# Weight sums made by adding transfers in DRAM, a new order of first use, and a last product cut in column halves

## The chip, the cores and the metric

The kernel runs on one core of one Trainium2 chip. TensorE multiplies, VectorE (DVE), ScalarE (ACT) and GpSimd (POOL) work on tiles in the on-chip memory, SyncE (SP) issues most transfers. The metric is the device time of one execution in microseconds; the median of 3 runs is 2372.4 (2371.81 to 2376.11).

## The reference

One decoder layer on 512 tokens, model width 2048, in float32:

```
h = RMSNorm(x); z = h @ W_in          # q, k, v of 8 attention heads; q, k, v, gate of 8 retention heads
a = block-sparse causal attention (QK-RMSNorm, rotary);  r = silu(gate) * groupnorm(retention)
x += concat(a, r) @ W_o
x += (silu(h2 @ W_gate) * (h2 @ W_up)) @ W_down      # h2 = RMSNorm(x), inner width 5632
x += (p @ W_pp) * sigmoid(RMSNorm(x) @ W_pg + b_pg)
```

## The kernel before

Every product keeps float32 accuracy by splitting each operand into a rounded part H and a rest L (`split`, L51: ScalarE makes H, VectorE makes L) and multiplying three times (`mm3`, L72: H by H, H by L, L by H).

The large products after the first go through seven multiplications of half-size blocks instead of eight. A `Group` (L245) computes 512 rows by 1024 columns over 2 to 4 units of depth 512. Its seven products come in the order of `ORDER` (L112): 1, 5, 6, 3, 7, 2, 4. One step is one product of one unit: 12 matmuls of 512 columns. The weight side of each product is a quarter of the weights or a sum of quarters: product 1 uses quarter 11; 5 is 11 + 12; 6 adds 22; 3 uses 22; 7 is 12 + 22; 2 uses 21; 4 adds 21 to the sum of 6. `add` (L269) makes these sums on VectorE in place, in the tile `raw` of 128 x 1024 numbers, by `plus` (L80, the group "raw<-raw" of L81). So a unit has four loads of 512 KB and four sums. The activation side of each product, its "factors" (`factors`, L173), is made on VectorE and ScalarE from transposed chunks, and either stays in tiles s and r or is spilled to DRAM through the four buffers of the tile o (`spill`, L194) and reloaded (`reload`, L225).

`run` (L148) goes through the list of steps; at step i it calls `extract` (the split) for step i + 2, `add` for step i + 3 and `multiply` for step i. Tile places the instructions on each engine by a simulation of its own, except where `keep_in_program_order` pins them. The raw tiles have three tags of four buffers each (l1, bd, c). The split tiles wh and wl have three buffers.

In order of time: the head (about 0 to 53 us by the trace), where class `Plain` (L452) multiplies the first q and k columns directly while x is loaded, scaled and split (`h_chunk` L499, `first_factors` L506, driven by `beside` L543); three groups for the values and gates; the mixer (about 285 to 720 us), where the projections of the heads run beside attention and retention, with one call of `weights` (L610) per unit of depth 256; two groups with W_o; eleven groups gu0 to gu10 with W_gate and W_up (L1025; gu0's first steps go unit by unit, in the order of `in_units`, because its factors are only being made); six groups with W_down in three parts of depth (L1031), the last part with 3 units; and two groups with W_pg (L1073; called pl0 and pl1 here). `evacuate` (L320) brings results out of the accumulation banks X, Y, Z; `gate` (L1050) finishes the output. Twenty idle matmuls on zeros (L449) stand before the first real one.

## Time and profile before

| | us |
|---|---|
| median of the three runs | 2372.4 |
| the profiled execution: its span, first to last instruction | 2367.2 |
| TensorE busy in it | 2317.0 |
| VectorE busy | 1943.3 |
| ScalarE busy | 1197.7 |
| GpSimd busy | 61.9 |

The profile is one execution; "busy" counts the time in which at least one instruction of the engine ran. Matmuls are pipelined, so TensorE can be busy and yet not at its peak. What waits for what is read from the semaphores; a wait is put down to what came last.

### The profile page before, as it was taken

The page shows a single profiled execution, that of the slowest core. Times are in us where ns is not written, and L with a number is a line of the kernel's source. Part 1 is how long each engine was busy: PE and PEld are TensorE (multiplying, and loading weights), DVE is VectorE, ACT ScalarE, POOL GpSimd, SP SyncE. Part 2 cuts the span into 40 slices and gives each one's busy share as a digit, 9 for nine tenths or more (in the row PEclk, how much of TensorE's full clock was granted, in tenths as well). Part 3 has the DMA queues.
Part 4 walks back from the last instruction along what each step waited for, and adds up shares of the span by engine and source line. Part 5 has one row for each costly group of instructions (what it writes and reads, how often), then busy time and mean ns, then how long its engine had stood idle before and what let it go on. Part 6 is the DMA issues. An engine that isn't in the chain of part 4 may idle for free.

```text
span 2367.2 us, 29161 instructions
## 1 busy us (share of the span) xinstructions
PE 2317.0 (98%) x10480; PEld 1898.7 (80%) x10480; DVE 1943.3 (82%) x2626; ACT 1197.7 (51%) x1791; POOL 61.9 (3%) x47
## 2 busy tenths in 40 slices
PE   9999999999999999999999999999999999999898
PEld 7888877788877877888888888888888878887777
DVE  8888686666667998888988898888888878789997
ACT  7644454444455565544554455445544434356653
POOL 0000011100010002000000000000000000000000
PEclk9999999999999999999999999999999999999999
DMA  6634733345666694346434643464577856857463
GB/s 233 241 130 162 233 104 123 129 149 182 195 216 257 231 346 160 109 163 201 147 111 156 200 152 111 151 200 155 204 322 253 290 219 235 331 183 259 137 204 124
DMA packets 166529, 456.26 MB, mean 193 GB/s; under 512 B 18544, under 2 KB 31216, under 8 KB 162288
## 3 DMA queue, kind: packets, MB, share of 16 engines
q1 hardware_dynamic: 162400, 446.00, 55.3%
q10 hardware_dynamic: 2704, 4.20, 0.7%
q0 software_dynamic: 1280, 4.20, 0.5%
q8 instruction: 82, 1.34, 0.2%
q14 instruction: 63, 0.52, 0.1%
HBM read 348.42 MB, written 101.71 MB: 190 GB/s over the span
## 4 chain that ended last, share of the span: by engine, by line
issue 57%; PE 26%; DVE 10%; DMA 5%; ACT 1%; POOL 1%; SPq 0%; ACTq 0%; POOLq 0%; DVEq 0%
PE acc L63 10%; PE Y L63 6%; PE Z L63 4%; DVE wl L55 3%; PE at L63 3%; DVE raw L81 2%; PE X L63 2%; DMA h<-o 1%; ACT wh L54 1%; PE tp L68 1%; DMA pp<-pp 1%; POOL rstd L84 1%; DMA s<-h 0%; DMA mix<-o 0%; DVE o L55 0%
## 5 line engine op out<-in xcount | busy, mean ns | idle before, releaser
L54 ACT ACTIVATE wh<-raw 128x1024 fp32r<-128x1024 f32 (+1 forms) x728 | 769.5, 1059 | 866.0 <-PE Y L63 307.8
L55 DVE TENSOR_TENSOR wl<-raw,wh 128x1024 fp32r<-128x1024 f32 (+1 forms) x728 | 884.4, 1218 | 281.4 <-ACT wh L54 280.5
L63 PE MATMUL Y<-wh,s 128*128 128x512 f32 x1656 | 525.6, 391 | 5.5 <-DVE v L78 3.2
L81 DVE TENSOR_TENSOR raw<-raw 128x1024 f32<-128x1024 f32 x376 | 453.2, 1217 | 20.1 <-DMA raw<-in_w_gu 7.2
L63 PEld LDWEIGHTS Y<-wh,s 128*128 128x128 f32 x1656 | 310.9, 188 | 72.9 <-ACT wh L54 5.4
L63 PE MATMUL Z<-wh,s 128*128 128x512 f32 x1152 | 365.1, 390 | 0.3 <-ACT wh L54 0.2
L63 PE MATMUL X<-wh,s 128*128 128x512 f32 x1008 | 320.9, 392 | 7.5 <-ACT wh L54 4.7
L63 PE MATMUL Y<-wl,s 128*128 128x512 f32 x828 | 324.8, 392 | 1.1 <-DVE wl L55 0.9
L63 PEld LDWEIGHTS Z<-wh,s 128*128 128x128 f32 x1152 | 216.2, 188 | 45.6 <-ACT wh L54 1.2
L63 PE MATMUL Z<-wl,s 128*128 128x512 f32 x576 | 228.0, 396 | 4.5 <-DVE wl L55 4.5
L63 PEld LDWEIGHTS X<-wh,s 128*128 128x128 f32 x1008 | 189.6, 189 | 49.1 <-ACT wh L54 6.7
L63 PE MATMUL X<-wl,s 128*128 128x512 f32 x504 | 197.8, 392 | 0.8 <-DVE wl L55 0.8
L63 PEld LDWEIGHTS Y<-wl,s 128*128 128x128 f32 x828 | 155.9, 188 | 34.8 <-DVE wl L55 2.9
L63 PE MATMUL Y<-wh,r 128*128 128x512 f32 x504 | 167.4, 393 | 2.2 <-ACT wh L54 2.1
L63 PE MATMUL acc<-h,wh 128*128 128x512 f32 x512 | 160.3, 394 | 0.8 <-DVE m L721 0.8
L63 PEld LDWEIGHTS Z<-wl,s 128*128 128x128 f32 x576 | 108.2, 188 | 29.6 <-DVE wl L55 7.7
L63 PE MATMUL acc<-wh,h 128*128 128x512 f32 x384 | 130.1, 398 | 1.4 <-DVE m L721 1.1
L63 PE MATMUL Z<-wh,r 128*128 128x512 f32 x352 | 116.1, 390 | 0.2 <-ACT wh L54 0.2
L63 PEld LDWEIGHTS Y<-wh,r 128*128 128x128 f32 x504 | 95.1, 189 | 22.9 <-ACT wh L54 3.5
L63 PEld LDWEIGHTS X<-wl,s 128*128 128x128 f32 x504 | 95.0, 189 | 21.1 <-DVE wl L55 1.7
L63 PEld LDWEIGHTS acc<-h,wh 128*128 128x128 f32 x512 | 92.4, 188 | 17.7 <-issue 1.4
L63 PE MATMUL Y<-wl,r 128*128 128x512 f32 x252 | 100.2, 398 | 0.5 <-DVE wl L55 0.5
(212 smaller groups left out, 2842.8 us busy)
## 6 DMA issues: line engine op xcount, KB each, us to landing
raw<-in_w_gu SPq DMA_DIRECT2D x176, 512.0 KB, 4.3
raw<-in_w_dn SPq DMA_DIRECT2D x88, 512.0 KB, 6.0
a<-o SPq DMA_DIRECT2D x154, 256.0 KB, 2.9
raw<-in_wqk SPq DMA_DIRECT2D x63, 512.0 KB, 3.7
s<-a SPq DMA_DIRECT2D x21, 1536.0 KB, 7.5
raw<-in_w_vg SPq DMA_DIRECT2D x48, 512.0 KB, 5.0
raw<-in_w_ow SPq DMA_DIRECT2D x32, 512.0 KB, 5.4
xin<-x SPq DMA_DIRECT2D x64, 256.0 KB, 5.3
```

The source lines that it names most:

```text
L54: return (nc.scalar.activation(H, src, AF.Copy), nc.vector.tensor_tensor(L, src, H.bitcast(F32), op=ALU.subtract))
L55: nc.vector.tensor_tensor(L, src, H.bitcast(F32), op=ALU.subtract))
L63: ins = nc.tensor.matmul(*args, **kw)
L68: ins = nc.tensor.transpose(o, a, ident)
L81: nc.vector.tensor_tensor(o, a, b, op=ALU.add)
L84: nc.gpsimd.tensor_tensor(dst, src, neghalf[:, :1].to_broadcast([P, n]), op=ALU.pow)
```

## The change

Three groups (gu0; the second column group of W_down's last depth part, "dn" here; pl0) get `sums`: the sums of their weight quarters are made in DRAM by transfers on GpSimd's queue. `summed` lists, for each of the products 5, 7, 6, 4 and each unit, a copy and then an adding transfer, 512 KB each. The 32 of gu0 go out one per unit of the mixer from slot 41 on; the 24 of dn and 32 of pl0 go out at six steps of each group from gu0 on. Each waits (`paced`) for a ScalarE split. These groups load each product's weights by a transfer of their own, seven per unit, and `add` does nothing.

In the head, the first unit's two weight halves and the first two chunks of x are issued alternately and pinned, H is made straight from the loaded chunk, the first two units multiply by operand and not by row block, the factors come two steps later, and 9 idle matmuls stand instead of 20. In the tail, pl1's last product keeps program order; its second row block is accumulated in two column halves in two banks, with the third and fourth unit at the end; `ending` writes out the order of the last operations, and the last four pairs of operands are loaded into raw buffers early.

```diff
@@ -137,7 +137,27 @@
     QUARTER = {"3": (0, 1), "7": (1, 1), "2": (0, 0), "4": (1, 0)}
+    def paced(ins, by):
+        tc.add_manual_dep(ins.ins, by.ins.name, mybir.DependencyInfo(mybir.DependencyClass.Sync, mybir.DependencyReason.DATA),
+                          reason="paced")
+    def summed(name, src, units):
+        sums, moves = {}, []
+        for p, base, more in (("5", (0, 0), (0, 1)), ("7", (0, 1), (1, 1)), ("6", "5", (1, 1)), ("4", "6", (1, 0))):
+            sums[p] = [dram.tile([P, 2 * T + 64], F32, name=f"{name}{p}_{u}")[:, :2 * T]
+                       .rearrange("p (c n) -> p c n", c=2) for u in units]
+            for add in range(2):
+                for u, k in enumerate(units):
+                    of = src(*more, k) if add else sums[base][u] if base in sums else src(*base, k)
+                    moves.append((sums[p][u], of, {"accum_op": ALU.add} if add else {}))
+        return sums, moves
+    def move(m, behind):
+        paced(nc.gpsimd.dma_start(m[0], m[1], **m[2]), behind)
     now = [0]
+    lead = [None]
@@ -243,18 +263,26 @@
     class Group:
-        def __init__(self, src, units, tiles, evac, order=None, after=lambda p: None, ready=lambda p, u: None):
+        def __init__(self, src, units, tiles, evac, order=None, after=lambda p: None, ready=lambda p, u: None, sums=None):
+            self.sums = sums
...
             self.raw, self.bank, self.w, self.next = {}, {}, {}, None
-            self.pinned = False
+            self.pinned = self.ends = False
...
         def load(self, q, u):
-            t = rawq.tile([P, 2, T], F32, name="raw", tag={"11": "l1", "12": "bd"}.get(q, "c"))
-            ins = nc.sync.dma_start(t, self.src(int(q[0]) - 1, int(q[1]) - 1, self.units[u]))
+            where = None
+            tag = {"11": "l1", "12": "bd"}.get(q, "c")
+            if self.sums:
+                q = {"11": "1", "12": "5", "22": "6"}.get(q, q)
+                tag = {"5": "bd", "7": "bd", "6": "c", "2": "c"}.get(q, "l1")
+                where = self.sums[q][u] if q in self.sums else None
+            a = SOURCE.get(q, q)
+            t = rawq.tile([P, 2, T], F32, name="raw", tag=tag)
+            ins = nc.sync.dma_start(t, self.src(int(a[0]) - 1, int(a[1]) - 1, self.units[u]) if where is None else where)
@@ -268,6 +296,8 @@
             r = lambda q: self.raw[q, u]
+            if self.sums:
+                return
@@ -282,8 +312,13 @@
             wl = wq.tile([P, 2, T], F32R, name="wl", tag="wl")
-            parts = split(wh, wl, self.raw[SOURCE[p], u])
+            parts = split(wh, wl, self.raw[p if self.sums else SOURCE[p], u])
+            lead[0] = parts[0]
             self.w[p, u] = wh, wl
+            if self.sums and p in "1563":
+                self.load({"1": "3", "5": "7", "6": "2", "3": "4"}[p], u)
+            if self.sums and p == "2":
+                self.load_next("22", u)
@@ -300,12 +335,23 @@
             last = self.left[p] == 0
-            for b in range(2):
+            self.w[u] = wh, wl
+            whole, lo, hi = (0, T), (0, T // 2), (T // 2, T)
+            todo = [(0, u, whole), (1, u, whole)]
+            if self.ends and p == "4":
+                todo = [(0, u, whole)]
+                if first:
+                    self.bank["H"] = pools["chain"].tile([P, T], F32, name="Z1", tag="Z1")
+                for c in (lo, hi) if self.left[p] != 1 else ():
+                    todo += [(1, v, c) for v in ((u - 1, u) if last else (u,))]
+            in_order[0] = in_order[0] or self.ends and p == "4"
+            for b, v, (c0, c1) in todo:
                 at = slice(b * P, (b + 1) * P)
+                to = self.bank["H"] if c0 else self.bank[k][b]
                 for c in range(2):
-                    s = self.tiles[p].pair(2 * u + c)
-                    mm3(self.bank[k][b], s[:, 0, at], s[:, 1, at], wh[:, c, :], wl[:, c, :],
-                        first and c == 0, last and c == 1, p in "237")
+                    s = self.tiles[p].pair(2 * v + c)
+                    mm3(to[:, :c1 - c0], s[:, 0, at], s[:, 1, at], *(x[:, c, c0:c1] for x in self.w[v]),
+                        first and c == 0, last and v == u and c == 1, p in "237")
@@ -446,7 +492,7 @@
     idle = tp_p.tile([P, T], F32, name="tp", tag="tp")
-    for _ in range(20):
+    for _ in range(9):
@@ -457,27 +503,36 @@
             self.raw[u] = rawq.tile([P, 2, T], F32, name="raw", tag="l1" if u < 4 else "c")
-            if u == 0:
-                for c in range(2):
-                    tc.keep_in_program_order(nc.sync.dma_start(self.raw[u][:, c], wqk[0, u, :, c]))
-            else:
+            if u:
                 tc.keep_in_program_order(nc.sync.dma_start(self.raw[u], wqk[0, u]))
+        def start(self, c):
+            tc.keep_in_program_order(nc.sync.dma_start(self.raw[0][:, c], wqk[0, 0, :, c]))
+            if c == 0:
+                self.w[0] = [wq.tile([P, 2, T], F32R, name=n, tag=n) for n in ("wh", "wl")]
+            for ins in split(*(w[:, c] for w in self.w[0]), self.raw[0][:, c]):
+                tc.keep_in_program_order(ins)
...
         def extract(self, p, u):
-            self.w[u] = [wq.tile([P, 2, T], F32R, name=n, tag=n) for n in ("wh", "wl")]
             if u:
+                self.w[u] = [wq.tile([P, 2, T], F32R, name=n, tag=n) for n in ("wh", "wl")]
                 return split(*self.w[u], self.raw[u])
-            for c in range(2):
-                split(*(w[:, c] for w in self.w[u]), self.raw[u][:, c])
...
             wh, wl = self.w.pop(u)
-            for b in range(NB):
+            for c in range(2 if u < 2 else 0):
+                k = 2 * u + c
+                for x, w in ((0, wh), (0, wl), (1, wh)):
+                    for b in range(NB):
+                        matmul(self.acc[b], h[:, k, x, b * P:(b + 1) * P], w[:, c, :],
+                               start=k == 0 and not x and w is wh, stop=False)
+            for b in range(NB if u > 1 else 0):
@@ -500,7 +555,10 @@
         tc.keep_in_program_order(ins)
-        nc.scalar.activation(t, t, AF.Copy, scale=gm[:, k:k + 1])
+        pin = tc.keep_in_program_order if k < 2 else lambda ins: None
+        pin(nc.scalar.activation(h[:, k, 0, :], t, AF.Copy, scale=gm[:, k:k + 1]))
+        pin(nc.scalar.activation(t, t, AF.Copy, scale=gm[:, k:k + 1]))
+        pin(nc.vector.tensor_tensor(h[:, k, 1, :], t, h[:, k, 0, :].bitcast(F32), op=ALU.subtract))
@@ -548,15 +606,15 @@
                 first.load(0)
+            else:
+                first.load(i + 2)
...
             for k in (2 * i + 4, 2 * i + 5):
-                t = h_chunk(k)
-                split(h[:, k, 0, :], h[:, k, 1, :], t)
-                chunks[i + 2].append(t)
-            if i > -2:
-                first.load(i + 2)
-        if 0 <= i + 1 < NC // 2:
-            first_factors(i + 1, chunks.pop(i + 1))
+                if i == -2:
+                    first.start(k)
+                chunks[i + 2].append(h_chunk(k))
+        if 0 <= i - 1 < NC // 2:
+            first_factors(i - 1, chunks.pop(i - 1))
@@ -586,6 +644,7 @@
     pieces = {}
+    s_gu, gu_moves = summed("sgu", lambda kh, nh, u: w_gu[0, kh, nh, u], range(4))
@@ -614,8 +673,10 @@
             nc.sync.dma_start(raw, stream.pop(0))
-            split(wh, wl, raw)
+            made = split(wh, wl, raw)
             ready.append((wh, wl))
+            if gu_moves and slot[0] > 40:
+                move(gu_moves.pop(0), made[0])
@@ -1025,7 +1082,8 @@
                             None if j else in_units(((0, 1), (3,), (2,))),
-                            reload(s_d[0], s_a[0], KG[0]) if j == FS - 1 else lambda p: None))
+                            reload(s_d[0], s_a[0], KG[0]) if j == FS - 1 else lambda p: None,
+                            sums=None if j else s_gu))
@@ -1038,6 +1096,11 @@
+    s_dn, late = summed("sdn", lambda kh, nh, u: w_dn[1, kh, nh, u], range(first[2], first[3]))
+    s_pl, more = summed("spl", lambda kh, nh, u: w_pl[0, kh, nh, u], range(4))
+    late += more
+    groups[-1].sums = s_dn
@@ -1047,12 +1110,57 @@
+    coming = {}
+    def get(t, tb, s):
+        nc.sync.dma_start(t[0], xd[3][tb][:, s])
+        nc.sync.dma_start(t[1], ppd[tb][:, s])
+    held = []
+    def ending(b, o, t, bank, to):
+        if b == 0:
+            held.extend((o, t, bank, to))
+            return
+        r = lambda b: rstd[2][:, 2 + b:3 + b]
+        pin = tc.keep_in_program_order
+        whole, lo, hi = slice(0, T), slice(0, T // 2), slice(T // 2, T)
+        def opened(o, c, of, b):
+            pin(nc.vector.scalar_tensor_tensor(o[:, c], of, r(b), o[:, c], op0=ALU.mult, op1=ALU.add))
+            nc.scalar.activation(o[:, c], o[:, c], AF.Sigmoid)
+        def times(o, c, t):
+            pin(nc.vector.tensor_tensor(o[:, c], o[:, c], t[1][:, c], op=ALU.mult))
+        def closed(o, c, t, to):
+            pin(nc.vector.tensor_tensor(o[:, c], o[:, c], t[0][:, c], op=ALU.add))
+            nc.sync.dma_start(to(c), o[:, c])
+        o0, t0, bank0, to0 = held
+        opened(o0, whole, bank0, 0)
+        times(o0, whole, t0)
+        opened(o, lo, bank[:, lo], 1)
+        closed(o0, whole, t0, to0)
+        times(o, lo, t)
+        opened(o, hi, groups[-1].bank["H"][:, lo], 1)
+        closed(o, lo, t, to)
+        times(o, hi, t)
+        closed(o, hi, t, to)
...
             tb, s = 2 * th + b, 2 * n + nh
+            if (tb, s) in coming:
+                return coming.pop((tb, s))
             t = [ev_tile("g", 4, name="xin"), ev_tile("g", 4, name="pp")]
-            nc.sync.dma_start(t[0], xd[3][tb][:, s])
-            nc.sync.dma_start(t[1], ppd[tb][:, s])
+            get(t, tb, s)
+            if n == 1 and (tb, s) == (NB - 1, NS - 1):
+                for r in range(NB):
+                    both = rawq.tile([P, 2, T], F32, name="both", tag="bd")
+                    coming[r, s - 1] = both[:, 0], both[:, 1]
+                    get(coming[r, s - 1], r, s - 1)
@@ -1061,6 +1169,9 @@
             tb, s = 2 * th + b, 2 * n + nh
+            if n == 1 and bank is not None:
+                ending(b, part, t, bank, lambda c: out[tb * P:(tb + 1) * P, s * T + c.start:s * T + c.stop])
+                return
@@ -1072,12 +1183,16 @@
         groups.append(Group(lambda kh, nh, u, n=n: w_pl[n, kh, nh, u], range(4), s_e, gate(n),
-                            None if n else in_units(((0, 1), (3,), (2,)))))
+                            None if n else in_units(((0, 1), (3,), (2,))), sums=None if n else s_pl))
+    groups[-1].ends = True
...
         take_over(i)
+        j, k = divmod(i - 56, 28)
+        if j >= 0 and k in (8, 11, 14, 17, 20, 23) and late:
+            move(late.pop(0), lead[0])
```

More of the change, by code (lines that the diff above doesn't have):

```diff
@@ L893, in back @@
         return s_o[p].load(pairs.start, s_mix[p][:, pairs])
-    def paced(ins, by):
-        tc.add_manual_dep(ins.ins, by.ins.name, mybir.DependencyInfo(mybir.DependencyClass.Sync, mybir.DependencyReason.DATA),
-                          reason="paced")
     s_o = {}
```

## The prediction

> **What bounds the kernel now.** I read the page first, then the stretches between the stages, then what TensorE waits for in them.
>
> ```profile
> span 2367.2 us, 29161 instructions
> PE 2317.0 (98%) x10480; PEld 1898.7 (80%) x10480; DVE 1943.3 (82%) x2626; ACT 1197.7 (51%) x1791; POOL 61.9 (3%) x47
> L81 DVE TENSOR_TENSOR raw<-raw 128x1024 f32<-128x1024 f32 x376 | 453.2, 1217 | 20.1 <-DMA raw<-in_w_gu 7.2
> ...
> 2357.95 0.39 PE L63 MATMUL Y<-wl,s 128*128 128x512 f32 x1
> 2358.17 0.39 PE L63 MATMUL Y<-wh,s 128*128 128x512 f32 x1
> ```
>
> TensorE is the bound: 98% of the span. Two matmuls in a row start 0.22 us apart, though each lasts 0.39, so "busy" hides lost slots and I count matmuls instead. VectorE at 82% is the next engine, and 376 weight sums of 1.217 us are a quarter of it. Four stretches by the windows view: a steady one inside group gu1..gu9, and the opening steps of the three groups that the change touches.
>
> ```profile
> 1179.05:1219.42 40.37, 40.37 (x183) 33.42 (x182) 32.44 (x33) 19.78 (x23) 0.00 (x0) 1.00 0.35 115
> 880.93:921.30 40.37, 34.98 (x149) 25.68 (x148) 38.54 (x61) 22.47 (x43) 13.63 (x1) 1.00 0.48 192
> 2120.00:2163.43 43.43, 39.65 (x185) 31.91 (x183) 41.94 (x62) 30.09 (x56) 0.00 (x0) 1.00 0.65 225
> 2190.49:2232.34 41.85, 35.73 (x157) 27.82 (x155) 39.77 (x72) 25.67 (x52) 3.93 (x1) 0.96 0.39 122
> ```
>
> The columns are TensorE, weight loads, VectorE, ScalarE, GpSimd (busy us and count), granted clock, DMA share, GB/s. The steady stretch has 183 matmuls in 40.37 us, 0.2206 each. At that rate the other three lose (183 - 149) x 0.2206 = 7.5 us (gu0), 43.43 - 185 x 0.2206 = 2.6 (second product group of w_dn's last third, dn), and 41.85 - 157 x 0.2206 = 7.2 (pl0). Dn's count is flattered by short transposes; TensorE's idle time there is 43.43 - 39.65 = 3.8, and half a clock follows the stall (3.50 us at 0.51, worth 1.7), so I use 5.5.
>
> ```profile
> 2163.00:2166.50 3.50, 3.07 (x7) 2.48 (x8) 3.50 (x8) 0.92 (x3) 0.00 (x0) 0.51 0.98 348
> ...
> PE Y L63 <- DVE v L78: 3.2, 1, 3.2
> PE X L63 <- ACT wh L54: 2.9, 2, 2.7
> PE Z L63 <- DVE wl L55: 2.2, 1, 2.2
> ...
> ACT wh L54 <- DVE raw L81: 14.0, 7, 3.7
> ```
>
> The first three waits are TensorE's from 2120 to 2232, the last is ScalarE's from 880 to 960: where ACT is named, ACT itself waited for a sum on VectorE. VectorE is 95 to 97% busy in all three. So the loss of some 20 us is VectorE's, and it sits where factors are made beside the sums.
>
> **The change, part by part.**
>
> *Sums off VectorE.* Groups gu0, dn and pl0 lose four sums per unit: 16 + 12 + 16 = 44 x 1.217 = 53.5 us of VectorE. In the bound stretches:
>
> ```profile
> L81 DVE TENSOR_TENSOR raw<-raw 128x1024 f32<-128x1024 f32 x12 | 14.6, 1214 | 0.1
> ...
> L81 DVE TENSOR_TENSOR raw<-raw 128x1024 f32<-128x1024 f32 x12 | 14.6, 1217 | 0.2 <-DMA raw<-in_w_dn 0.2
> ...
> L81 DVE TENSOR_TENSOR raw<-raw 128x1024 f32<-128x1024 f32 x11 | 13.4, 1214 | 0.0
> ```
>
> Gu0: VectorE keeps 38.54 - 14.6 = 23.9 us for 32.9 us of TensorE work, 73%; the steady stretch lives at 80% without a stall. Dn: 27.3 in about 38, 72%. Pl0: 26.4 in 34.7, 76%. VectorE stops being the bound. What stays are short chains (a transpose waits for its bank, a bank for its copy), and in dn and pl0 the transfers are next. I take 6 of 7.5, 3.5 of 5.5 and 5 of 7.2: **14.5 us**. Bounds: 5 (order, not load, made most stalls) to 20.2.
>
> *Seven loads per unit instead of four.* 33 more of 512 KB, issued on SP when the split of an earlier product frees the buffer. SP waits in this way already:
>
> ```profile
> SPq L257 <- DVE wl L55: 58.7, 17, 26.2
> ```
>
> That is 17 loads between 840 and 960 us that stood on SP until a split had freed their buffer. Queued behind such a wait are factor stores and residual loads; the new loads hang on splits that are made at the pace of TensorE, so a wait lasts a step at most. The load of the next group's third quarter moves from the last product's sum to the split of "2", three steps earlier: no cost. Each new load is asked for some nine steps before its use (9 x 2.7 us), and lands in 4.3 us by the row below, so cover is ample; dn's window, at share 0.65, gets about 9 x 0.5 MB more, to some 0.9, which is why I take least there.
>
> *The transfers that make the sums.* 88 on GpSimd's queue: 32 in the mixer, one per unit, and 56 in gu0 to gu9, six per group. No row shows a transfer from DRAM to DRAM or one that adds. Nearest rows:
>
> ```profile
> pp<-pp POOLq DMA_DIRECT2D x16, 256.0 KB, 6.6
> raw<-in_w_gu SPq DMA_DIRECT2D x176, 512.0 KB, 4.3
> ...
> 360.00:590.00 230.00, 224.61 (x1101) 185.28 (x1100) 158.81 (x357) 107.85 (x221) 15.88 (x10) 1.00 0.47 146
> 960.00:1640.00 680.00, 679.33 (x3057) 560.23 (x3057) 586.81 (x700) 342.96 (x458) 0.00 (x0) 1.00 0.46 151
> ...
> ACT o L54 <- DMA mix<-o: 10.3, 7, 2.6
> ACT o L54 <- DMA a<-o: 14.1, 12, 2.7
> DVE raw L81 <- DMA raw<-in_w_gu: 6.4, 10, 1.4
> ACT z L735 <- POOL rs L84: 8.8, 9, 2.0
> ```
>
> 146 GB/s at share 0.47 is 310 GB/s in full use: 512 KB take 1.7 us of all engines, 3.4 if an adding one reads twice. The mixer goes from 0.47 to 0.7 or 0.9, the gu groups to 0.6 or 0.7: it fits. What can pay are the last four rows, transfers and a GpSimd result for which an engine already waits with nothing in hand: 7 + 12 + 10 + 9 = 38 waits between 340 and 1700 us. Behind a waiting transfer on GpSimd stand only the small powers (the last row). TensorE works two steps behind the splits (5.4 us), which hides most of a lengthening. The powers get a second delay of their own: a move stands before them until the ScalarE split that paces it is done; that split is made in the same step, so it is late by a step at most, and the keys' scaling that needs the power is used many steps on. Lower bound 0; upper bound all 38 waits (10.3 + 14.1 + 6.4 + 8.8 = 39.6 us) doubled and passed on in full: 40. The steady stretch shows 40.37 of 40.37 busy although such waits occur in it, so I stay near the low end: **+2 us**. The Trainium skill ("DMA: Bandwidth & Descriptors", section on the anatomy of a GpSimd-issued DMA) gives 2.0 us plus bytes over 436 GB/s, an estimate of 3.2 us for such a move; the pp row, 6.6 us for half the bytes amid other traffic, is slower, and the sum would be the same by either.
>
> *Head.*
>
> ```profile
> 1.23 6.75 PE L450 MATMUL tp<-zeros 128*128 128x512 bf16 x20 [1.23 <-DVE zeros L445]
> 8.02 0.50 PE L63 MATMUL Y<-wh,h 128*128 128x512 f32 x1
> 10.86 0.39 PE L63 MATMUL Y<-wl,h 128*128 128x512 f32 x1
> ...
> 5.47 0.15 PEld L450 LDWEIGHTS <-zeros 128*128 128x128 bf16 x1 [0.27 <-issue]
> 5.88 1.61 PEld L450 LDWEIGHTS <-zeros 128*128 128x128 bf16 x8 [0.26 <-issue]
> ...
> 3.81 1.30 ACT L54 ACTIVATE wh<-raw 128x512 fp32r<-128x512 f32 x2 [1.02 <-DMA raw<-in_wqk]
> 5.58 0.72 ACT L503 ACTIVATE x<-x,gm 128x512 f32<-128x512 f32 x1 [0.47 <-DMA x<-in_xT]
> ```
>
> Seven real matmuls start before 10.86 (one at 8.02, six more up to 10.63); from there on they run without a gap. That equals a gapless start at 10.86 - 7 x 0.227 = 9.27. Afterwards x comes second in the queue (landing between 4.5, where the second weight half lands now, and 5.5), ScalarE makes H directly in 0.72, and matmuls go H by wh, H by wl, L by wh, so L has four more matmuls' time. Nine idle matmuls at 0.42 us end at 5.1. First real one at 5.3 to 6.2, I take 5.9, then no gap: -3.4; less 0.4 for a late L or split: **-3**. Factors made two steps later cost nothing: their first use is after product 1 of the next group.
>
> *Tail.*
>
> ```profile
> 2358.60 0.75 DVE L1065 SCALAR_TENSOR_TENSOR e<-Y,rstd,e 128x512 f32<-128x512 f32 x1 [0.38 <-PE Y L63]
> 2359.38 0.63 ACT L1067 ACTIVATE e<-e 128x512 f32<-128x512 f32 x1 [0.50 <-DVE e L1065]
> 2362.43 0.69 DVE L1068 TENSOR_TENSOR e<-e,pp 128x512 f32<-128x512 f32 x1 [1.49 <-DMA pp<-pp]
> 2363.15 0.69 DVE L81 TENSOR_TENSOR e<-e,xin 128x512 f32<-128x512 f32 x1
> ...
> L63 PE MATMUL at<-v,PL 128*128 128x256 f32 x80 | 19.7, 282 | 0.0
> ```
>
> From the last matmul's start to the end are 2367.2 - 2358.17 = 9.0 us; 1.49 of them is a late load, which the early buffers remove. VectorE's nine pinned operations (0.75 + 2 x 0.69, and six halves at about 0.42) begin some 2.4 us before the last matmul's start, when the first bank is whole, and with two waits for a sigmoid (0.63, a half 0.4) end about 3.0 after it; the store and the end take 2367.2 - 2363.84 = 3.4 now, about 3.2 for half of it: 6.2. A 256-wide matmul costs 282 - (390 - 227) = 119 ns, so 48 for 24 add 48 x 0.119 - 24 x 0.227 = 0.3. **-2.5**; bounds -1 to -4.
>
> **Sum.** -14.5 + 2 - 3 - 2.5 = -18: a span of 2349.2. The median, 2372.4, lies 5.2 above the span, and I keep that: **2354**.
>
> **Rivals.**
> - *All comes back*: -20.2 - 3.4 - 3 with moves free, 26.6 in all: about 2346. For it: VectorE at 73 to 76%.
> - *Order or transfers, not VectorE's load*: 5 of the 14.5 come back: -5 - 3 - 2.5 + 2 = -8.5, 2364. For it: PE Y <- DVE v, 3.2, hangs on a copy that ScalarE placed late, and DMA share 0.98 beside it.
> - *Slower: the moves lengthen waits.* The 38 waits double and TensorE takes all of it: +39.6 against 20 won, 2392. It decides from 20 / 38 = 0.53 us per wait on. For it: in the steady groups the load for product 4 lands as VectorE asks for it, and moves fall in those steps. Against it: 5.4 us of work in hand at TensorE.
> - *Cold start*: idle matmuls run 0.42 us apart until 5.47 and at full speed from 5.88. If nine, ended at 5.1, leave the array slow for one stretch more (3.4 us at half, like the row at 2163), the loss is 1.7: 2356. The Trainium skill ("TensorE: Matmul & The Clock Gate", Part 1) says that the clock opens after a busy window of about 3.4 us whose phase is free; both rows fit it.
>
> **How the numbers follow.** Forecast 0.42 (own range 2349 to 2360); all back 0.15; order 0.23; moves 0.09; cold 0.11. The range 2344 to 2367 leaves out the moves case and the outer parts of two others. A measurement tells about 0.2% (4.7 us) from no change: faster 0.86, same 0.05 (the upper part of the order case), slower 0.09.
>
> **What would show it.** Right: the three windows hold near 183 matmuls per 40.4 us with no raw sums in them, VectorE below 85%, the first gapless matmul near 6 us, 6 to 6.5 us after the last one. Wrong: the waits of ScalarE on mix<-o or a<-o, of VectorE on raw and of ScalarE on rs grow by over half a us each, steady gu groups lengthen, or dn waits for raw loads.

## The result, and the profile after

The changed kernel takes 2347.4 us (median of four runs, 2346.4 to 2348.4) against 2372.4 (four runs): a ratio of 0.9895, 95% interval 0.9883 to 0.9907. The forecast was 2354 with a range of 2344 to 2367. It came true in sign and cause; several of its terms did not have the right size, and the time lies below the range of its main case (2349 to 2360). Of the kernels below, two had one slow execution each (8601.5 and 4533.4 us), which their medians and ratios leave out.

From the page of the changed kernel:

```profile
span 2344.6 us, 29412 instructions
...
PE 2307.3 (98%) x10493; PEld 1897.4 (81%) x10493; DVE 1896.3 (81%) x2585; ACT 1199.6 (51%) x1792; POOL 105.3 (4%) x135
```

and from its groups by line, shapes apart (count, busy us, mean ns, idle time before):

```profile
L81 DVE TENSOR_TENSOR raw<-raw 128x1024 f32<-128x1024 f32 x332 | 400.4, 1219 | 16.4 <-DMA raw<-in_w_dn 5.4 <-DMA raw<-in_w_vg 4.1 <-DMA raw<-in_w_gu 2.5
```

The 44 sums are gone (376 became 332), and TensorE is busy for 98% as before: the share can't show what happened, since matmuls overlap (each lasts 0.39 us, and the next starts after 0.23): a matmul that starts late leaves no idle time until the one before it has ended. What shows it is the length of each stage, measured from the same matmul in both traces. The marks are the first matmul of a group's product 2 (bank X), for the mixer's end that of W_o's first product, in pl0 that of product 3 (bank Z), the fourth of its seven, and for the tail the last matmul's start.

| stage, us | before | after | difference |
|---|---|---|---|
| to product 2 of the third value group (head) | 261.88 | 260.51 | -1.4 |
| rest of that group, mixer | 450.93 | 455.90 | +5.0 |
| W_o, to product 2 of its second group | 142.19 | 142.21 | 0.0 |
| end of W_o, gu0 to its product 2 ("gu0" below) | 91.45 | 85.33 | -6.1 |
| end of gu0, gu1 to gu10, W_down's first two groups ("the steady groups") | 939.06 | 937.62 | -1.4 |
| W_down's next groups | 220.67 | 219.03 | -1.6 |
| end of the group before dn, dn, pl0's first three products ("dn and pl0") | 129.79 | 113.77 | -16.0 |
| pl0's last four products, pl1 ("pl1") | 122.19 | 124.25 | +2.1 |
| tail | 9.02 | 5.99 | -3.0 |
| sum (span) | 2367.2 | 2344.6 | -22.6 |

The steady groups and W_down's next groups show 3.0 us less together. Traces of kernels that are alike in these two stages spread by 2.5 and 2.8 us in them, so no gain is shown there.

The windows view has the three stages that count, first of before, then of after (the columns as in the prediction):

```profile
261.88:712.81 450.93, 436.80 (x2125) 361.19 (x2123) 308.06 (x646) 217.52 (x437) 38.01 (x34) 1.00 0.53 166
855.01:946.46 91.45, 85.68 (x379) 67.34 (x378) 81.00 (x116) 51.79 (x89) 13.63 (x1) 1.00 0.66 244
2106.19:2235.99 129.80, 119.37 (x534) 95.63 (x533) 119.74 (x184) 81.41 (x147) 3.93 (x1) 0.97 0.61 205
```

```profile
260.51:716.40 455.89, 438.33 (x2125) 360.84 (x2123) 307.75 (x646) 217.36 (x437) 58.87 (x66) 1.00 0.67 201
858.62:943.95 85.33, 83.32 (x380) 67.81 (x379) 64.18 (x101) 51.67 (x89) 4.35 (x6) 1.00 0.97 364
2100.60:2214.37 113.77, 113.77 (x533) 94.11 (x532) 94.69 (x160) 80.85 (x147) 1.03 (x1) 1.00 0.95 335
```

Read the stage of dn and pl0, the last row of each: the same matmuls, 533 or 534, in 16 us less. TensorE had no idle time left in them (113.77 of 113.77), the clock that was 0.97 is 1.00, and VectorE went from 92% to 83% of the stretch. The transfers are at 0.95 of what 16 engines give, and TensorE still waited for none. In gu0 VectorE went from 89% to 75%. The first rows are the loss: in the mixer the same 2125 matmuls take 5 us more, with the DMA share up from 0.53 to 0.67. The waits view of the mixer says where, before and after:

```profile
DVE zr L816 <- DMA mr<-zr: 12.3, 4, 4.8
ACT z L735 <- POOL rs L84: 12.0, 11, 2.0
...
ACT o L54 <- DMA mix<-o: 11.5, 8, 2.6
```

```profile
DVE zr L877 <- DMA mr<-zr: 18.7, 5, 7.8
...
ACT o L54 <- DMA mix<-o: 14.7, 11, 2.8
ACT z L796 <- POOL rs L84: 14.4, 11, 2.0
```

Sum in us, number, longest: three waits that were there before (35.8 us together) are 47.8 us. The largest growth is at mr<-zr, 128 KB that ScalarE's queue fetches for retention; it landed in 3.7 us before and in 5.5 now (medians of 24 in this stage). Other loads land later too: the stage's weights (raw<-in_wqk) after 4.6 us instead of 3.6. TensorE stands idle for 17.6 us of the stage, 14.1 before; which of the waits it pays for is not traced.

The tail, from the timeline of the changed kernel:

```profile
2338.62 0.28 PE L63 MATMUL Z<-wh,s 128*128 128x256 f32 x1
...
2340.87 0.43 DVE L1138 TENSOR_TENSOR e<-e,both 128x256 f32<-128x256 f32 x1
```

VectorE ends 2.7 us after the last matmul's start (5.7 before), with no wait for a load. In the head the first matmul of the product starts at 5.55 us, 0.31 after the idle ones end, and the next ones follow without a wait, until:

```profile
16.99 0.39 PE L63 MATMUL Y<-wl,h 128*128 128x512 f32 x1
19.09 0.74 PE L63 MATMUL Y<-wh,h 128*128 128x512 f32 x2 [1.71 <-DVE h L561]
```

### The profile page after: what moved, and what is told of

It reads as the page before. It is cut to its first block, busy times and chain, and to the rows that moved or that the text cites. A ratio compares the mean times of both kernels' runs of the same rounds, so it can differ in the third digit from the quotient of the medians.

```text
span 2344.6 us, 29412 instructions
## 1 busy us (share of the span) xinstructions
PE 2307.3 (98%) x10493; PEld 1897.4 (81%) x10493; DVE 1896.3 (81%) x2585; ACT 1199.6 (51%) x1792; POOL 105.3 (4%) x135
## 4 chain that ended last, share of the span: by engine, by line
PE 56%; DMA 2%; DVE 2%; issue 1%; ACT 0%; SPq 0%; ACTq 0%; DVEq 0%
PE Y L63 24%; PE Z L63 16%; PE X L63 15%; PE tp L68 1%; DMA x<-xin 1%; DMA xin<-x 1%; DVE wl L55 1%; DMA a<-o 1%; DVE raw L81 0%; ACT wh L54 0%; DMA pp<-pp 0%; DVE e L81 0%; DVE e L78 0%; DVE e L1176 0%; DVE e L1131 0%
## 5 line engine op out<-in xcount | busy, mean ns | idle before, releaser
L63 PE MATMUL Y<-wh,s 128*128 128x512 f32 (+1 forms) x1656 | 522.9, 389 | 0.5 <-ACT wh L54 0.5
L81 DVE TENSOR_TENSOR raw<-raw 128x1024 f32<-128x1024 f32 x332 | 400.4, 1219 | 16.4 <-DMA raw<-in_w_dn 5.4
L63 PE MATMUL Z<-wh,s 128*128 128x512 f32 (+1 forms) x1164 | 368.6, 390 | 0.2 <-ACT wh L54 0.2
L63 PE MATMUL Y<-wl,s 128*128 128x512 f32 (+1 forms) x828 | 323.4, 391 | 0.2 <-DVE wl L55 0.2
L63 PE MATMUL Z<-wl,s 128*128 128x512 f32 (+1 forms) x582 | 229.7, 395 | 2.1 <-DVE wl L55 2.1
L63 PE MATMUL Z<-wh,r 128*128 128x512 f32 (+1 forms) x356 | 116.7, 388 | 0.0
L63 PE MATMUL acc<-h,wl 128*128 128x512 f32 x256 | 100.3, 392 | 0.0
```

What stands on the lines that cost most here:

```text
L63: ins = nc.tensor.matmul(*args, **kw)
L81: nc.vector.tensor_tensor(o, a, b, op=ALU.add)
```

## The experiments

Each kernel is the changed one with an edit of its own. The times, with the ratio to the kernel before on the same chip:

| kernel | median us | ratio, 95% interval |
|---|---|---|
| idle VectorE work in the sums' place | 2366.0 | 0.9975, 0.9965 to 0.9985 |
| dn's and pl0's sums on VectorE | 2361.7 | 0.9953, 0.9936 to 0.9970 |
| gu0's sums on VectorE | 2351.4 | 0.9908, 0.9893 to 0.9923 |
| gu0's transfers ahead of the mixer | 2349.9 | 0.9899, 0.9885 to 0.9914 |
| gu0's transfers early in the mixer | 2347.5 | 0.9897, 0.9882 to 0.9912 |
| transfers in the steady groups doubled | 2350.2 | 0.9903, 0.9888 to 0.9918 |
| head's new order for four units | 2345.4 | 0.9882, 0.9867 to 0.9898 |
| head of before | 2347.4 | 0.9892, 0.9877 to 0.9906 |
| tail of before | 2348.5 | 0.9897, 0.9880 to 0.9913 |
| pl1's sums in DRAM too | 2354.5 | 0.9926, 0.9911 to 0.9942 |
| the same, transfers in pairs | 2350.5 | 0.9909, 0.9894 to 0.9924 |
| three edits together | 2343.6 | 0.9884, 0.9864 to 0.9903 |

An interval is 5 to 9 us wide, so edits of 1 to 5 us are read by the stages of their traces, which are far steadier: dn and pl0 took 113.77 us in all eleven traces that keep the change's sums there without added VectorE work.

### Was it VectorE's load?

```diff
             if self.sums:
+                if p in "5674":
+                    nc.vector.tensor_tensor(r(p), r(p), r(p), op=ALU.max)
                 return
```

> The changed kernel, with one VectorE operation of the old sums' size and place (the maximum of a tile with itself, which leaves it as it is) before each of the 44 splits that a sum stood before, in gu0, dn and pl0. Transfers, loads, buffers and order of the program stay those of the changed kernel. Theory (VectorE's load made the lost slots): all three stretches lengthen by what they had gained in the trace: gu0 by 6, dn by 6, pl0 by 10 us, so a span near 2344.6 + 22 = 2366. Rival (the loads' order or the earlier loads made them): 0 to 5 us, a span of 2345 to 2350.

Measured: gu0 91.9 us (+6.5 on the changed kernel), dn and pl0 122.1 (+8.4), the rest of pl0 and pl1 125.4 (+1.1). The windows of the first two, and, from the groups by line in the second of them, the operation that was added:

```profile
859.67:951.55 91.88, 85.70 (x380) 69.18 (x378) 81.89 (x117) 52.27 (x89) 4.35 (x6) 0.98 0.93 333
2110.23:2232.37 122.14, 117.89 (x533) 94.51 (x532) 116.07 (x182) 79.75 (x148) 1.03 (x1) 0.99 0.91 315
```

```profile
L301 DVE TENSOR_TENSOR raw<-raw 128x1024 f32<-128x1024 f32 x20 | 24.3, 1217 | 2.6 <-DMA raw<-spl 2.5
```

All loads, transfers and buffers are the changed kernel's, only 1.217 us of VectorE stand again before each split. All that gu0 had won is gone, and over half of what dn and pl0 had. The theory holds, but by 16 us in the traces' stages (18.5 between the medians), not by 22; the other half of dn and pl0 needs a second cause. The added operation stands between a load and its split, as the sum did: the run shows what work on VectorE costs at that place, but doesn't tell VectorE's time from the longer chain.

### Dn and pl0 as before

```diff
-    s_dn, late = summed("sdn", lambda kh, nh, u: w_dn[1, kh, nh, u], range(first[2], first[3]))
-    s_pl, more = summed("spl", lambda kh, nh, u: w_pl[0, kh, nh, u], range(4))
-    late += more
+    s_dn, s_pl, late = None, None, []
```

> The changed kernel with dn's and pl0's sums back on VectorE, as before the change, with their four loads for a unit, and without the 56 transfers in the steady groups. From the end of the group ahead of dn to the first partial product of pl0's last product the changed kernel takes 113.8 us, before 129.8, and the run with idle VectorE work in the sums' place took 9.5 more than the changed one. Theory A (VectorE's time and the order and loads that hang on the sums cost together): the full 16 come back, a span near 2361. Theory B (only VectorE's time is the change's doing, the other 6.5 were the luck of one schedule): 9 to 11, near 2355. For the transfers: the steady groups gu1 to gu10 stay within 1.5 us of the changed kernel's if they were free.

```profile
2103.62:2234.13 130.51, 120.76 (x533) 96.87 (x532) 119.81 (x184) 81.47 (x147) 3.25 (x1) 0.96 0.60 204
```

```profile
PE Z L63 <- DVE wl L55: 4.3, 2, 2.2
PE Y L63 <- DVE v L78: 3.5, 1, 3.5
```

These are the window and the two longest of TensorE's waits in it. The whole loss is back, 130.5 us, with the wait for v on VectorE (3.5; it was 3.2 before) and a lower clock behind the stops (0.96, as 0.97 before). So it was no luck of one schedule. (What the expectation calls the first partial product of pl0's last product is product 3, the fourth of seven.) The first run has no such wait and a clock of 0.99: 3.5 us of stop and 0.03 x 130.5 = 3.9 us of clock make up most of the 8.4 that the added work didn't bring back. What places the copy of v late when the sums are on VectorE (the order in which the instructions are placed, or the loads) isn't settled. The steady groups, here without the 56 transfers (51 of them in this stage, 5 in gu0's), take 938.6 us, against 937.6 to 940.1 in the eight traces with the 56 alone: within that spread they are free.

### The mixer's five microseconds

```diff
-    s_gu, gu_moves = summed("sgu", lambda kh, nh, u: w_gu[0, kh, nh, u], range(4))
+    s_gu, gu_moves = None, []
```

> The changed kernel without the part for gu0: its 32 transfers in the mixer are gone, and its sums are back on VectorE. Theory (the transfers delay the mixer's small ones: mr<-zr lands in 6.6 us in place of 3.7): the mixer gives back its 5 us, gu0 costs its 6 again: +1, a span near 2345.6. Rival (the mixer's 5 us have another cause, as a drift from run to run or the order of the head): the mixer stays, gu0 costs 6: +6, near 2351.

The stage takes 452.1 us (-3.8), gu0 91.9 (+6.5). The transfers do it. Then they were put ahead of the mixer:

```diff
...
     def beside(i):
+        if i >= 26 and i % 2 == 0 and gu_moves:
+            move(gu_moves.pop(0), lead[0])
...
-            if gu_moves and slot[0] > 40:
-                move(gu_moves.pop(0), made[0])
```

> The changed kernel with gu0's 32 transfers not in the mixer but before it, in the second half of the groups for the decays and values, one in every second step, paced by the last split. Theory (as for the kernel without them): -4 to -5, a span near 2340, mr<-zr back at 3.7 us, and no cost where they stand now, as TensorE works there on weights that were loaded well ahead. Rival 1 (another cause): 0. Rival 2 (wherever they stand, something waits): the mixer's 5 us come back and 3 to 5 are lost in the value groups: about 0.

The mixer falls to 450.6 us, and the value groups pay: 267.7 to the third group's mark in place of 260.5. In their waits view, from 106 to 268 us, stand a wait that the changed kernel hasn't at all, one that was 3.1 there and one that was 0.3:

```profile
ACT wh L54 <- DMA raw<-in_w_vg: 9.9, 6, 2.8
DVE raw L81 <- DMA raw<-in_w_vg: 9.0, 6, 4.9
...
ACT vH L56 <- DVE v L81: 5.2, 1, 5.2
```

The second rival was right: the price moved with the transfers, and rose. Next, inside the mixer but done before mr<-zr is asked for:

```diff
-            if gu_moves and slot[0] > 40:
-                move(gu_moves.pop(0), made[0])
+            for _ in range(2 if 40 < slot[0] < 60 else 1):
+                if gu_moves:
+                    move(gu_moves.pop(0), made[0])
```

> The changed kernel with gu0's 32 transfers from the mixer's first weight unit on, two for a unit at a few units, so that the last starts before the first retention product's small loads (mr<-zr, at 510 us). Theory (the mixer's loss is the doubling of these loads alone, since up to 530 us the kernels with and without transfers stand level): the mixer gives back 3 of its 3.6 us, a span near 2341.5, mr<-zr at 3.7 us. Rival (at the mixer's start stand loads that are as late, as in the groups for the values, where the same 32 cost 7.2): what is won at 530 is lost before 360, 0 to +3.

456.8 us: nothing won. The waits of the stage:

```profile
ACT z L797 <- POOL rs L84: 18.4, 14, 4.1
...
ACT o L54 <- DMA mix<-o: 13.0, 9, 3.1
DVE zr L878 <- DMA mr<-zr: 11.4, 5, 4.6
```

mr<-zr is back at its old 11 to 12 us, and z's wait for the powers, which GpSimd makes on the queue that also issues the transfers, grew from 12.0 to 18.4. The last run (below) avoids both places, and there the third wait grew, for mix<-o, from 11.5 to 20.2. The three waits and the stage, by kernel:

| transfers | mr<-zr | z <- rs | mix<-o | sum | stage us |
|---|---|---|---|---|---|
| none (before) | 12.3 | 12.0 | 11.5 | 35.8 | 450.9 |
| none (gu0's sums on VectorE) | 12.3 | 12.0 | 12.2 | 36.5 | 452.1 |
| ahead of the mixer | 12.2 | 12.0 | 11.4 | 35.6 | 450.6 |
| the changed kernel's | 18.7 | 14.4 | 14.7 | 47.8 | 455.9 |
| early in the mixer | 11.4 | 18.4 | 13.0 | 42.8 | 456.8 |
| around retention's loads | 12.8 | 14.1 | 20.2 | 47.1 | 456.7 |

With the transfers wherever in the mixer, the sum is 7 to 12 us larger and the stage some 5 longer. All nine traces with them in their first place lie between 454.5 and 457.0. My theory of one bad place (retention's loads) fell: in their first place 32 transfers cost 4.6 us on average in this stage, 0.14 each, in the other two places some 5.5, and the wait that grows changes with the place.

### Are the transfers in the steady groups free?

```diff
...
             move(late.pop(0), lead[0])
+            move((spare.pop(0), w_dn[1, 0, 0, 0], {}), lead[0])
```

> The changed kernel, with a second transfer of 512 KB from DRAM to DRAM (a part of W_down into a spare tile) right behind each of the 56 transfers in the steady groups. Theory (transfers in steps without factor stores are hidden): 0 to +1 us. Rival (they are paid in part, below what one trace can tell): the cost of a transfer shows, +0.05 us or more for each, +3 and above, in gu1 to gu10.

The stage of the steady groups takes 942.8 us, 5.1 more than in the changed kernel and 3.9 more than the mean of eight traces with 56 transfers (938.8). From the waits view between 945 and 1725 us, the changed kernel and this one:

```profile
ACT o L54 <- DMA a<-o: 25.6, 27, 2.8
...
DVE raw L81 <- DMA raw<-in_w_gu: 2.5, 4, 1.4
ACT wh L54 <- DMA raw<-in_w_gu: 1.9, 1, 1.9
```

```profile
ACT o L54 <- DMA a<-o: 42.7, 34, 3.7
...
ACT wh L54 <- DMA raw<-in_w_gu: 21.2, 10, 3.8
...
DVE raw L81 <- DMA raw<-in_w_gu: 6.6, 8, 1.9
```

With one transfer every 8 us ScalarE's wait for a<-o had already grown from 14.8 to 25.6, and TensorE, two steps behind the splits, took nothing of it. With two at a time the raw loads themselves come late (21.2), and TensorE pays. The rival was right for the second 56, the theory for the first.

### Head and tail

```diff
-            for c in range(2 if u < 2 else 0):
+            for c in range(2 if u < 4 else 0):
...
-            for b in range(NB if u > 1 else 0):
+            for b in range(NB if u > 3 else 0):
```

> The changed kernel with the head's order of operands (H by wh, H by wl, L by wh for a chunk) for the first four units in place of the first two. Theory (the stall of 1.7 us at 17.0 us comes from unit 2, which goes bank by bank and so needs L of both of its chunks at once): the stall goes or falls to 0.3, -1.4 us, a span near 2343.2. Rival (ScalarE and VectorE are simply behind there, and the wait moves on to H of the next unit): 0 to -0.5.

The stop at 17 us is gone; the timeline at that place shows pairs of matmuls without a wait:

```profile
16.70 0.62 PE L63 MATMUL Z<-wh,h 128*128 128x512 f32 x2
17.15 0.61 PE L63 MATMUL Y<-wh,h 128*128 128x512 f32 x2
17.61 0.62 PE L63 MATMUL Z<-wh,h 128*128 128x512 f32 x2
```

The mark at 51.45 us is reached at 49.84, 1.6 us earlier, and 1.3 are left at the next groups. The theory holds. With the head of before in the changed kernel (its 20 idle matmuls, bank by bank, factors through a rounded copy):

```diff
-    for _ in range(9):
+    for _ in range(20):
...
```

> The changed kernel with the head of before (20 idle matmuls, weights by way of the queue ahead of x, both halves of a factor from a rounded copy, bank by bank). Theory: the change's head is worth what the traces' positions show, 1.4 us: a span near 2346. Rival (worth the 3 us of the prediction, with something lost behind the head): near 2347.6, and the positions of the later stages as in the changed kernel less 1.4.

The marks are 1.6 to 2.0 us later: the change's head is worth that, not 3. In the median it doesn't show. With the tail of before:

```diff
-            if n == 1 and (tb, s) == (NB - 1, NS - 1):
+            if False:
...
-            if n == 1 and bank is not None:
+            if False:
...
-    groups[-1].ends = True
```

> The changed kernel with the tail of before (last product unit by unit, both banks whole at the end, the last loads of residual and gate in their turn). Theory: the tail is worth the 3.0 us of the traces (9.03 to 5.99 us after the last matmul's start), a span near 2347.6, and e<-e,pp waits 1.5 us for its load again. Rival: the load comes in time now that VectorE makes no sums at the end of pl0, and only 1.5 us come back, 2346.1.

```profile
2338.04 0.39 PE L63 MATMUL Y<-wh,s 128*128 128x512 f32 x1
...
2341.56 0.69 DVE L1179 TENSOR_TENSOR e<-e,pp 128x512 f32<-128x512 f32 x1 [1.02 <-DMA pp<-pp]
```

8.2 us from the last matmul's start to the end, against 6.0: the tail is worth 2.2 here, and the wait for pp is 1.0 in place of 1.5. Theory and rival each got a part of it.

### One group more, and a version of three edits

```diff
+    s_p1, more = summed("sp1", lambda kh, nh, u: w_pl[1, kh, nh, u], range(4))
+    late += more
...
-        if j >= 0 and k in (8, 11, 14, 17, 20, 23) and late:
+        if j >= 0 and k in (5, 8, 11, 14, 17, 20, 23, 26) and late:
```

> The changed kernel with pl1's sums made by transfers in DRAM too (32 more in the steady groups, eight for a group in place of six). Theory (VectorE's sums are what pl1 still waits for at 2276 us, 1.5 us of stalls and 1.5 to 2 us of half clock behind them): -2 to -3.5, a span near 2341.8. Rival (the four raw loads more for a unit, beside the gate's and residual's loads, take the place of the sums, or the steady groups pay for the closer transfers): 0 to +2.

The stage of pl1 falls from 124.3 to 119.9 us, as the theory says. But the steady groups take 951.3 (+13.7), nearly all of it in one stop of 7.6 us at 1751 us and, within 60 us behind it, a stretch of half clock and smaller stops. ScalarE's and TensorE's waits there, and the issues of 1725 to 1745 us:

```profile
ACT wh L54 <- DMA raw<-in_w_dn: 16.9, 2, 14.1
...
PE X L63 <- ACT wh L54: 7.6, 1, 7.6
```

```profile
s<-a SPq DMA_DIRECT2D x2, 1536.0 KB, 16.9
raw<-in_w_dn SPq DMA_DIRECT2D x5, 512.0 KB, 16.2
sp<-in_w_pl POOLq DMA_DIRECT2D x3, 512.0 KB, 8.8
```

Three of the last transfers meet the factor loads of W_down's first groups; a raw load lands after 16.2 us. Between the same times in the changed kernel, with no transfer of GpSimd's, it lands after 10.5 (median of 7). In pairs, done sooner:

```diff
...
-        if j >= 0 and k in (8, 11, 14, 17, 20, 23) and late:
-            move(late.pop(0), lead[0])
+        if j >= 0 and k in (8, 11, 14, 17, 20, 23):
+            for _ in range(2 if k < 18 else 1):
+                if late:
+                    move(late.pop(0), lead[0])
```

> The changed kernel with pl1's sums in DRAM too, but the transfers in pairs at four of the six steps of a steady group, so that all 88 are made before the first groups of W_down, where the ones at the end of the wider schedule met 15 us loads and a stop of 7.8 us. Theory (the stop came from those transfers; pl1 itself won 4.3 us): pl1's 4.3 less 32 times the 0.05 us that a doubled transfer cost: -2 to -3, a span near 2342. Rival (the stop is from other causes, or pairs cost as much): 0 to +3.

No stop at 1751 us, and pl1 at 119.9 us, but the steady groups take 944.1 (+6.5), all of it in their first half, where two thirds of the transfers are. ScalarE's wait for a<-o between 945 and 1725 us is 58.4 (25.6 in the changed kernel):

```profile
ACT o L54 <- DMA a<-o: 58.4, 36, 5.7
```

The last run has single transfers in every third step, nine in a group:

```diff
-            for c in range(2 if u < 2 else 0):
+            for c in range(2 if u < 4 else 0):
...
-            if gu_moves and slot[0] > 40:
+            n = slot[0]
+            if gu_moves and (24 < n < 122 or 170 < n < 182 or 190 < n):
...
-        if j >= 0 and k in (8, 11, 14, 17, 20, 23) and late:
+        if j >= 0 and k % 3 == 2 and late:
```

> Three edits to the changed kernel, in three stages that the trace tells apart. (1) The head's order of operands for four units. (2) gu0's 32 transfers from 330 us on in the mixer, none while the first two pairs' retention products are loaded for (about 508 to 595 us) nor at the third pair's (620 to 630 us). (3) pl1's sums in DRAM too, with one transfer in every third step of a steady group, nine in a group, so that all 88 have started by about 1700 us. Theory: (1) 1.6 us won at 51 us and kept; (2) the mixer within 1 us of the kernel without these transfers, 3 won, since each of the two losses seen so far stood at a load that an engine already waits for (mr<-zr from 510 us, the first transposes of z at 305 to 318 us); (3) no stop in W_down's first groups, 4 won in pl1. A span of 2336 to 2338. Rivals: (2) the eight transfers after 595 us cost what they cost before, 0 to 1 won; (3) nine in a group cost what pairs cost, 4 to 6 in gu1 to gu5, or the stop at 1751 us comes again: nothing won in sum, 2342 or more.

(1) held, 1.6 us at 260 us. (2) failed: 456.7 us. (3) held: the steady groups take 937.8 us with the 88 transfers (937.6 with the 56), and the stage of pl1 119.9. The windows from pl0's product 2 to the last matmul's start, in the changed kernel and in this one:

```profile
2236.13:2338.62 102.49, 100.79 (x457) 82.98 (x455) 91.87 (x107) 45.72 (x51) 0.00 (x0) 0.98 0.49 164
```

```profile
2236.61:2334.77 98.16, 98.16 (x457) 82.20 (x455) 74.92 (x91) 45.58 (x51) 0.00 (x0) 1.00 0.68 235
```

The same 457 matmuls in 4.3 us less, without idle time. The span is 2340.4 us and the median 2343.6, 3.8 below the changed kernel's. The intervals of the two ratios overlap, so the times alone don't prove the gain; the stages show where it comes from, 1.6 in the head and 4.3 in pl1, less 2.4 in W_down ahead of dn (221.5 us), a stage in which none of the edits works and the fourteen traces differ by 2.8.

## Why the prediction was right, and which sizes were off

The first point below rests on pl0's stretch from its first matmul to product 3, before and after:

```profile
2190.49:2235.99 45.50, 38.86 (x170) 30.11 (x169) 42.42 (x74) 29.32 (x57) 3.93 (x1) 0.96 0.36 113
```

```profile
2178.93:2214.37 35.44, 35.44 (x169) 29.42 (x168) 29.58 (x56) 26.80 (x51) 1.03 (x1) 1.00 0.91 319
```

- *Sums off VectorE, -14.5: the mechanism is right, the size too small.* Gu0 was put at 6 and gave 6.1. Dn and pl0 were put at 3.5 + 5 = 8.5 and gave 16.0. Two steps failed. The first is the count of lost slots by windows, 5.5 + 7.2: between equal matmuls the loss is 6.0 up to pl0's first matmul and 10.1 behind it, because pl0's window counted short transposes as full matmuls (157 x 0.2206 is 34.6 us, but the same stretch takes 32.7 in the changed kernel) and ended one step early. The second is the discount, 8.5 of 12.7, for order and transfers, which turned out to go with the sums: the wait for v, which I had set down for the rival, stays away in every trace without the sums and comes back with them.
- *Order, not load (2364): wrong as a rival, right as a part.* The added VectorE work alone brought back 6.5 + 8.4 us.
- *Seven loads and a DMA share near 0.9 in dn: no cost.* The share was 0.95, with TensorE never idle.
- *Transfers, +2: the mechanism of the slower rival, with 5.0 us of its 39.6.* In the mixer the three waits grew by 12.0 us and the stage by 5.0. My cover, two steps of work in hand, is that of the groups; I used it for the mixer too, where it did not hold. That the chains of attention and retention have less in hand is argued, not traced. The list of waits left out the one that grew most, mr<-zr, and my sign of trouble (over half a us more for each wait on the list) did not show: rs went from 1.1 to 1.3 us each, mix<-o from 1.4 to 1.3. For the steady groups the cover held: no cost with one transfer every third step, 3.9 us when doubled.
- *Head, -3: half.* The start at 5.9 was 5.55, without a cold start. The 0.4 us for "a late L or split" was a stop of 1.7 us: from unit 2 on the banks go one by one again, and the first needs L of both chunks at once.
- *Tail, -2.5: right.* It is -3.0 behind the last matmul's start, less 0.5 for the column halves (the last product takes 11.1 us up to that start, before 10.7; I had 0.3). With the tail of before in the changed kernel the part behind is -2.2.
- *The 5.2 us outside the span* were mostly not that: a later run of the kernel before took 2371.25 us with a span of 2369.2. The profiled execution was some 3 us faster than the median. Carried over, this made the forecast 3 us too long.
- *Not foreseen, and small: the stage of pl1 lost 2.1 us.* Of these, 0.5 are the column halves. Pl1's stops of 1.1 and 0.4 us for its sums, still on VectorE, stood there before too (1.0 and 0.4); new in this trace is the half clock behind them, which comes and goes from trace to trace (last section).
- *The total.* 2347.4 lies nearest to the rival "all comes back" (2346). That rival was right for the sums (22.1 us; it had 20.2), but not in its free transfers and whole head, so that its total fits is in part luck. So is it that the forecast missed by no more than 6.6 us: the sums were 7.6 too small, against 3.0 too little for the transfers and 1.6 too much for the head.

## What to carry to other kernels

Where an engine off the bound is over 90% busy in a stretch, measure the stretch between two equal matmuls of the bounding engine; counts in windows hide part of the loss (12.7 us counted, 16.0 lost here), because short transposes count as matmuls. Work that is moved into DRAM transfers is free where every consumer of a load has steps of work in hand, up to a rate (here one of 512 KB in 8 us; pairs were paid for), and costs at each short load for which an engine already waits: moving it past one such wait only finds the next.

## What the runs showed of the hardware

A short stop can be followed by half of TensorE's clock, and need not be. In the changed kernel two stops of 1.14 and 0.43 us, between 2275 and 2278 us, were followed by some 4 us at about half clock (the windows view, granted clock third from the right):

```profile
2276.00:2278.00 2.00, 1.05 (x3) 0.60 (x4) 2.00 (x3) 0.47 (x1) 0.00 (x0) 1.00 0.67 187
2278.00:2280.00 2.00, 2.00 (x7) 1.53 (x6) 2.00 (x3) 0.56 (x1) 0.00 (x0) 0.59 0.85 214
2280.00:2282.00 2.00, 2.00 (x7) 1.57 (x6) 2.00 (x2) 0.79 (x3) 0.00 (x0) 0.55 0.35 123
```

The same two stops stand in all eleven traces that keep pl1's sums on VectorE. Half a clock followed in four of them (0.52 to 0.59 for some 3 us or more) and not in the other seven, the kernel before among them (stops of 1.02 and 0.44 us, the second until 2298.62):

```profile
2298.00:2300.00 2.00, 1.56 (x7) 1.16 (x7) 2.00 (x3) 0.60 (x1) 0.00 (x0) 1.00 0.77 180
2300.00:2302.00 2.00, 1.66 (x8) 1.02 (x6) 2.00 (x3) 0.28 (x1) 0.00 (x0) 1.00 0.76 289
```

So the length of the stop alone doesn't decide it; what does is open. The stop of 1.71 us in the head had no such sequel either: its matmuls went on 0.23 us apart. The Trainium skill ("TensorE: Matmul & The Clock Gate", Part 1) has the clock fall after an idle window of about 3.4 us; these stops are shorter, together too, so here the measurement says that less idle time is enough at some times.

Transfers from DRAM to DRAM of 512 KB landed, in the changed kernel's mixer, after 6.3 us (24, 16 of them adding) and 5.4 us (8, from a sum):

```profile
sgu<-in_w_gu POOLq DMA_DIRECT2D x24, 512.0 KB, 6.3
...
sgu<-sgu POOLq DMA_DIRECT2D x8, 512.0 KB, 5.4
```

By the Trainium skill ("DMA: Bandwidth & Descriptors", section on the anatomy of a GpSimd-issued DMA) it would be an estimated 3.2 us; amid this kernel's other traffic neither of the two medians comes near it.
